# A gated conv and gMLP decoder layer in split fp32: loads of the first stage in a written order, the second half's row statistics from a token-major copy and spread through memory, weight remainders of v on GpSimd

## The chip, the cores and the metric

The kernel runs on one core of a Trainium2 chip. The metric is device time in microseconds (us) of one execution, and of a set of executions the median. The engines are PE (TensorE; PEld is its weight load), DVE (VectorE), ACT (ScalarE), POOL (GpSimd) and SP, which here only issues DMAs.

## The reference

One layer on `x` of 2048 tokens by 1024 channels, all in fp32, with a conditioning vector `c`:

```python
mod = c @ w_ada + b_ada
shift, scale, gate = split(mod, 3)
h = rmsnorm(x, g_pre) * (1 + scale) + shift
p = h @ w_in            # 8 parts of 1024 columns
y_a = conformer_conv(p[A.val], p[A.glu], p[A.silu])
v = layernorm(gelu(p[B.v]));  u = gelu(p[B.u])
y_b = (u * (tril(W_s) v + b_s) * silu(p[B.silu])) @ w_sgu_out
merged = sigmoid(p[gA]) * y_a + sigmoid(p[gB]) * y_b
out = rmsnorm(x + gate * (merged @ w_o), g_final)
```

`y_a` is a GLU, a causal depthwise convolution of width 31, a LayerNorm, a SiLU gate and a projection; the mixing by `W_s` goes per head in chunks of 128 tokens. What matters here is the head of this: the adaLN shift and scale, the RMS norm of x, and the product of h with the 1024 columns of v.

## The kernel before

The tokens go through in two passes (`s`) of 1024, each in two halves of T = 512. Channels are cut in KT = 8 tiles `k` of 128, a half in NC = 4 chunks `c` of 128 tokens. Every fp32 product is made of three fp32r products: each operand is split in a high part (a copy on ACT, L87) and a remainder (original minus high part, L88), and hi·hi, hi·lo and lo·hi are summed in PSUM. A step of the first stage is therefore 24 matmuls of 128x512: 4 chunks by 2 column halves by 3.

**The first stage (L455 to L563)** makes v for the first half of pass 0. It is written inside `tc.manual_schedule(engines=MANUAL)`, where PE, DVE, ACT and POOL run their instructions in the order in which the code is written. SP is not among them: its DMAs are put in order by the framework's scheduler. The stage does this:

- Loads: `xn` (x transposed, 8 tiles; L329), the row of c (`crow`), which PE multiplies by a column of ones to spread it over 128 partitions (L470, L473: `cbc`), per step two `wa` tiles of 512 KB (shift and scale weights, L381) and two pieces of the v weights (`raw`, 256 KB each, L174).
- Statistics of the first half: squares on ACT (L478, L481), a sum on DVE (L482), sums over partitions on PE (`col_sums`, L144), root and reciprocal (`rstd_cols`, L137, L138), and `spread` (L154, L161), which puts the 512 factors on all partitions by a diagonal and a matmul with ones.
- Per step k: `ada(k)` makes the shift and scale columns by two reductions of 128x1024 on DVE (L387) and an add (L391); `scaled(k)` multiplies xn by the row factors (L492); `shifted(k)` applies scale and shift twice on ACT (`modulated`, L352), once into the high part h, once in place; DVE makes the remainder of h (L516). The v weights are split on ACT (L87) and DVE (L88), a step ahead. Then 16 matmuls with the high part of h (L539, L540), 8 with its remainder (L544). Eight PSUM banks (`first`) hold the sums.
- The last step, k = 7, goes bank by bank (L552 to L554); `evict(u)` (L511) takes a bank through Gelu and gathers LayerNorm statistics.
- Beside it the second half's row statistics: squares of the transposed xn on ACT in steps 4 to 7 (L532), adds on DVE (L547, L548), `col_sums` after bank u = 5, then `spread` to `rx1`. `make_h` (L358, L352, L362) makes h of the second half, k = 0 in the stage, k = 1 to 7 behind it.

**Behind the stage** `v_pass` makes v of the second half from `A[1]`, once per column half n: 8 weight pieces of 12 matmuls each (L312 to L314). Its pieces are made by `make_row`, which splits them on ACT and DVE and sends each to memory (`d_wv`, issued on POOL, L186) for pass 1. The Gelu of column half n = 0 (L408) frees the banks for n = 1. Then follow the LayerNorm of v, the mixing, and the large products by quads (L297 to L303), whose order both versions share. `make_row` also makes the 16 pieces of `w_o`.

Three rings set what can run ahead: split weights `whl` (AHEAD + 1 = 5 tiles), `raw` (8), and the large ring `hs` (28 tiles of 512 KB), which holds h, wa, vn and the squares. Weights are prepared in the order of their use by `prep_to` and `take`.

Of the kernel before, what the change touches and what calls it, by code (L numbers as in the profile page):

```python
# [40 lines left out]
def hybrid_layer(  # L41
# [130 lines left out]
    def raw(mat, key, src):  # L172
        t = wp.tile([P, T], F32, tag="raw", name="raw", bufs=8)
        nc.sync.dma_start(out=t, in_=src)  # L174
        raws[key] = t
        return t

    def piece_tile():
        return wp.tile([P, 2, T], F32R, tag="whl", name="whl", bufs=AHEAD + 1)

    def make_row(mat, cache, k, n):
        def prep():
            w = piece_tile()
            split(w, raw(mat, None, mat[k * P : (k + 1) * P, n * T : (n + 1) * T]))
            if cache:
                nc.gpsimd.dma_start(  # L186
                    out=cache[k][n], in_=w.bitcast(F32).rearrange("p s c -> p (s c)")
                )
            return w

        return prep
# [185 lines left out]
    def load_ada(k):  # L377
# [4 lines left out]
            wa.append(t)  # L382
        return wa

    def ada(k, wa):
        for i in range(2):
            nc.vector.tensor_tensor_reduce(  # L387
                out=wa[i], in0=wa[i], in1=cbc, scale=col(V_GPRE, k) if i else 1.0, scalar=0.0,
                op0=ALU.mult, op1=ALU.add, accum_out=mod[:, k, i : i + 1],
            )  # L390
        nc.vector.tensor_tensor(out=mod[:, k], in0=mod[:, k], in1=base[:, k], op=ALU.add)  # L391


    def v_norm(vn, mv):
# [57 lines left out]


    xn = [xtile("xn") for _ in range(KT)]
    crow = row("crow")  # L455
    nc.sync.dma_start(out=crow[0:1, :], in_=rows[:, 3 * D : 4 * D])
    A = [[], []]
    load_xn(0, 0, xn)
    wa = {0: load_ada(0)}
    cbc = hs32("cbc")  # L460
    vn_first, st_first = v_tiles()
    with tc.manual_schedule(engines=MANUAL):
        nc.vector.tensor_copy(out=base[:, :, 0], in_=vec[:, V_BSH : V_BSH + KT])
        nc.vector.scalar_tensor_tensor(
            out=base[:, :, 1], in0=vec[:, V_BSC : V_BSC + KT], scalar=1.0,
            in1=vec[:, V_GPRE : V_GPRE + KT], op0=ALU.add, op1=ALU.mult,
        )
        for n in range(2):
            pt = bank()
            nc.tensor.matmul(  # L470
                pt, ones[0:1, :], crow[0:1, n * T : (n + 1) * T], start=True, stop=True
            )
            nc.scalar.activation(cbc[:, n * T : (n + 1) * T], pt, AF.Copy)  # L473
        acc = t512("acc")
        for k in range(KT):
            v = xn[k][:, :T]
            if k == 0:
                nc.scalar.activation(acc, v, AF.Square)  # L478
            else:
                q = t512("q")  # L480
                nc.scalar.activation(q, v, AF.Square)  # L481
                nc.vector.tensor_tensor(out=acc, in0=acc, in1=q, op=ALU.add)  # L482
        pc = bank()
        col_sums(acc, pc, 0, NC)
        prx = spread(rstd_cols(pc[:, :NC], NC), pc)
        rx = t512("rx")
        nc.scalar.activation(rx, prx, AF.Copy)
        ada(0, wa[0])

        def scaled(k):  # L490
            v = xn[k][:, :T]
            nc.vector.tensor_tensor(out=v, in0=v, in1=rx if k else prx, op=ALU.mult)  # L492

        def shifted(k):
            v = xn[k][:, :T]
            t = hs("h")
            modulated(t[:, 0], v, k)
            modulated(v, v, k)
            A[0].append(t)

        scaled(0)
        shifted(0)
        prep_to(2)
        cvt = wide()
        first = [bank() for _ in range(6)] + [cvt[:, :T], cvt[:, T:]]
        sq = []

        def evict(u):
            c, n = u // 2, u % 2
            vs = vn_first[c][:, n * T : (n + 1) * T]  # L510
            nc.scalar.activation(vs, first[u], AF.Gelu)  # L511
            nc.vector.bn_stats(out=st_first[c][:, n, :], in_=vs)

        for k in range(KT):
            t, v = A[0][k], xn[k][:, :T]
            nc.vector.tensor_tensor(  # L516
                out=t[:, 1], in0=v, in1=t[:, 0].bitcast(F32), op=ALU.subtract
            )
            ws = [ready.pop(0) for _ in range(2)]
            state["use"] += 2  # L520
            if k + 1 < KT:
                wa[k + 1] = load_ada(k + 1)
                scaled(k + 1)
                ada(k + 1, wa[k + 1])
                prep_to(2 * k + 4)
                shifted(k + 1)
            if k == 2:
                load_xn(0, 1, xn)
            if k >= 4:
                sq.append(hs32("q"))  # L530
                for i in range(2):
                    nc.scalar.activation(  # L532
                        sq[-1][:, i * T : (i + 1) * T], xn[2 * (k - 4) + i][:, T:S], AF.Square
                    )
            if k + 1 < KT:
                for u in range(2 * NC):
                    c, n = u // 2, u % 2
                    xh = t[:, 0, c * P : (c + 1) * P]
                    nc.tensor.matmul(first[u], xh, ws[n][:, 0], start=k == 0, stop=False)  # L539
                    nc.tensor.matmul(first[u], xh, ws[n][:, 1], start=False, stop=False)  # L540
                for u in range(2 * NC):
                    c, n = u // 2, u % 2
                    xl = t[:, 1, c * P : (c + 1) * P]
                    nc.tensor.matmul(first[u], xl, ws[n][:, 0], start=False, stop=False)  # L544
        tt = nc.vector.tensor_tensor
        for i in (1, 2, 3):
            tt(out=sq[0], in0=sq[0], in1=sq[i], op=ALU.add)  # L547
        tt(out=sq[0][:, :T], in0=sq[0][:, :T], in1=sq[0][:, T:], op=ALU.add)  # L548
        for u in range(2 * NC):
            c, n = u // 2, u % 2  # L550
            cs = slice(c * P, (c + 1) * P)
            nc.tensor.matmul(first[u], t[:, 0, cs], ws[n][:, 0], start=False, stop=False)  # L552
            nc.tensor.matmul(first[u], t[:, 0, cs], ws[n][:, 1], start=False, stop=False)
            nc.tensor.matmul(first[u], t[:, 1, cs], ws[n][:, 0], start=False, stop=True)  # L554
            if u < 2:
                evict(u)
            if u == 5:
                pc = bank()
                col_sums(sq[0], pc, 0, NC)
                c1 = rstd_cols(pc[:, :NC], NC)  # L560
        rx1 = spread(c1, pc)
        make_h(xn, rx1, 1, 0, A)
        for u in range(2, 2 * NC):  # L563
            evict(u)

    wsT = row("wsT")
    nc.sync.dma_start(out=wsT, in_=wst.rearrange("p j t -> p (j t)"))
# [22 lines left out]
    for s in range(NS):  # L590
        last = s + 1 == NS

        if s == 0:
            vn0, st0 = vn_first, st_first
            for k in range(1, KT):
                make_h(xn, rx1, 1, k, A)
        else:
            vn0, st0 = v_tiles()
# [532 lines left out]
```

## Time and profile before

| | |
|---|---|
| median of 3 runs | 1946.08 us (1945.91 to 1950.67) |
| profiled execution | 1949.32 us, of which the span is 1947.6 us |
| PE busy | 1859.1 us, 95% of the span |
| DVE, ACT, POOL busy | 1290.7, 867.6, 859.9 us |
| mean granted TensorE clock | 0.98 |
| DMA | 313.66 MB, mean 161 GB/s |

The span is the time between the profile's first and last instruction. A busy matmul of 128x512 at full clock comes every 0.22 to 0.23 us, though each lasts about 0.4: they overlap. Chain rows name what released each step of the path that ended last.

### The profile page before, as it was taken

How to read it: one execution, taken by the hardware profiler on the slowest of the kernel's cores; microseconds unless marked ns; L12 is line 12 of the kernel's file. 1: busy time of each engine (PE TensorE's matmuls, PEld its weight loads, DVE VectorE, ACT ScalarE, POOL GpSimd, SP SyncE). 2: the span in 40 equal slices, each digit the busy share in tenths (PEclk: the TensorE clock that was granted, in tenths of full speed). 3: DMA queues.
4: the chain of work that ended last, by engine and by line, in shares of the span. 5: the costliest groups of instructions: out<-in, count | busy, mean ns of one | idle time of the engine just before them, and what ended most of it. 6: DMA issues, size and time to landing. Idle time of an engine off the chain costs nothing.

```text
span 1947.6 us, 23204 instructions
## 1 busy us (share of the span) xinstructions
PE 1859.1 (95%) x8116; PEld 1517.4 (78%) x8116; DVE 1290.7 (66%) x1636; ACT 867.6 (45%) x1396; POOL 859.9 (44%) x734
## 2 busy tenths in 40 slices
PE   6798999999999998889999999999999999899998
PEld 4577888888888886668888878888888888677886
DVE  6776898888888127475851578889888861845424
ACT  4645555555546435322611455554555453532102
POOL 0035777777777710000100477777777774000000
PEclk9899999999999998889999999999999999899999
DMA  9562332222334384387886332333322246536484
GB/s 331 174 238 92 109 114 100 101 87 92 114 103 146 132 328 137 107 292 243 330 308 220 120 141 75 105 114 103 114 92 97 77 141 253 173 111 198 132 331 169
DMA packets 139015, 313.66 MB, mean 161 GB/s; under 512 B 15889, under 2 KB 16017, under 8 KB 138898
## 3 DMA queue, kind: packets, MB, share of 16 engines
q1 hardware_dynamic: 108434, 237.03, 36.2%
q0 software_dynamic: 11888, 41.43, 5.5%
q10 hardware_dynamic: 18576, 33.73, 4.6%
q8 instruction: 63, 1.03, 0.2%
q14 instruction: 54, 0.44, 0.1%
HBM read 226.66 MB, written 85.46 MB: 160 GB/s over the span
## 4 chain that ended last, share of the span: by engine, by line
PE 74%; issue 11%; DMA 7%; DVE 4%; ACT 3%; POOL 2%; SPq 0%; POOLq 0%; ACTq 0%; DVEq 0%
PE bank L297 21%; PE bank L300 21%; PE bank L303 21%; PE bank L312 3%; PE bank L313 3%; PE bank L314 3%; DMA wo<-d_wo 1%; PE bank L426 1%; DVE wa L387 1%; POOL whl L88 1%; DMA raw<-in_w_v 1%; DMA wa<-in_wada 1%; DMA xn<-in_xt 1%; DMA whl<-d_wo 1%; POOL raw L224 1%
## 5 line engine op out<-in xcount | busy, mean ns | idle before, releaser
L88 POOL TENSOR_TENSOR whl<-raw,whl 128x512 fp32r<-128x512 f32 x392 | 512.8, 1313 | 335.3 <-ACT whl L87 331.1
L704 DVE SCALAR_TENSOR_TENSOR cv<-a,vec,cv 128x1024 f32<-128x1024 f32 x464 | 596.6, 1286 | 31.6 <-ACT cv L698 21.4
L87 ACT ACTIVATE whl<-raw 128x512 fp32r<-128x512 f32 x504 | 314.3, 627 | 414.1 <-PE bank L303 214.7
L300 PE MATMUL bank<-s,whl 128*128 128x512 f32 x896 | 349.3, 390 | 1.7 <-DVE s L88 1.7
L303 PE MATMUL bank<-s,whl 128*128 128x512 f32 x896 | 349.7, 390 | 0.0
L297 PE MATMUL bank<-s,whl 128*128 128x512 f32 x896 | 349.4, 390 | 0.0
L224 POOL TENSOR_TENSOR raw<-raw 128x512 f32<-128x512 f32 x224 | 290.3, 1296 | 17.2
L297 PE MATMUL bank<-h,whl 128*128 128x512 f32 x672 | 264.0, 393 | 0.3 <-ACT bank L657 0.2
L300 PE MATMUL bank<-h,whl 128*128 128x512 f32 x672 | 261.8, 390 | 0.0
L303 PE MATMUL bank<-h,whl 128*128 128x512 f32 x672 | 261.6, 389 | 0.0
L300 PEld LDWEIGHTS bank<-s,whl 128*128 128x128 f32 x896 | 168.6, 188 | 38.0 <-DVE s L88 3.0
L297 PEld LDWEIGHTS bank<-s,whl 128*128 128x128 f32 x896 | 168.6, 188 | 34.9
L303 PEld LDWEIGHTS bank<-s,whl 128*128 128x128 f32 x896 | 168.7, 188 | 34.7
L297 PEld LDWEIGHTS bank<-h,whl 128*128 128x128 f32 x672 | 126.1, 188 | 32.5 <-DVE snap L680 5.3
L303 PEld LDWEIGHTS bank<-h,whl 128*128 128x128 f32 x672 | 126.1, 188 | 26.5
L300 PEld LDWEIGHTS bank<-h,whl 128*128 128x128 f32 x672 | 126.2, 188 | 25.6
L88 DVE TENSOR_TENSOR whl<-raw,whl 128x512 fp32r<-128x512 f32 x112 | 75.9, 688 | 96.9 <-ACT whl L87 91.8
L892 POOL DMA_DIRECT2D mb<-gl x32 | 17.3, 541 | 275.0 <-DVE gl L891 264.3
L297 PE MATMUL bank<-ya,whl 128*128 128x512 f32 x256 | 102.6, 401 | 13.8 <-ACT ya L87 10.6
L652 ACT ACTIVATE snap<-bank 128x512 f32<-128x512 f32 x112 | 66.5, 598 | 98.0 <-PE bank L303 98.0
L297 PE MATMUL bank<-yb,whl 128*128 128x512 f32 x256 | 105.4, 412 | 4.2 <-DVE gl L891 3.5
L300 PE MATMUL bank<-ya,whl 128*128 128x512 f32 x256 | 102.6, 401 | 1.4 <-DVE ya L88 1.4
(214 smaller groups left out, 2867.3 us busy)
## 6 DMA issues: line engine op xcount, KB each, us to landing
raw<-in_w_in SPq DMA_DIRECT2D x224, 256.0 KB, 3.0
yb<-yb SPq DMA_DIRECT2D x32, 512.0 KB, 7.6
whl<-d_wo SPq DMA_DIRECT2D x32, 512.0 KB, 4.6
whl<-d_wv SPq DMA_DIRECT2D x32, 512.0 KB, 4.3
xn<-in_xt SPq DMA_DIRECT2D x32, 256.0 KB, 5.4
wa<-in_wada SPq DMA_DIRECT2D x16, 512.0 KB, 6.5
raw<-in_w_v SPq DMA_DIRECT2D x32, 256.0 KB, 4.8
d_wv<-whl POOLq DMA_DIRECT2D x16, 512.0 KB, 6.5
```

The source lines that it names most:

```text
L87: nc.scalar.activation(hi, val, AF.Copy)
L88: eng.tensor_tensor(out=lo, in0=val, in1=hi.bitcast(F32), op=ALU.subtract)
L224: eng.tensor_tensor(out=dst, in0=dst, in1=src, op=ALU.add)
L297: nc.tensor.matmul(pt, wh, h[:, 0], start=start and k == 0, stop=False, skip_group_check=True)
L300: nc.tensor.matmul(pt, wh, h[:, 1], start=False, stop=False, skip_group_check=True)
L303: nc.tensor.matmul(pt, wl, h[:, 0], start=False, stop=k == last, skip_group_check=True)
L312: nc.tensor.matmul(pt, xh, w[:, 0], start=kt == 0, stop=False)
L313: nc.tensor.matmul(pt, xh, w[:, 1], start=False, stop=False)
L314: nc.tensor.matmul(pt, xl, w[:, 0], start=False, stop=kt == KT - 1)
L387: nc.vector.tensor_tensor_reduce(out=wa[i], in0=wa[i], in1=cbc, scale=col(V_GPRE, k) if i else 1.0, scalar=0.0, op0=ALU.mult, op1=ALU.add, ...
L652: nc.scalar.activation(t, pt, AF.Copy)
L704: nc.vector.scalar_tensor_tensor(out=dst, in0=a[:, k : k + S], scalar=col(V_CW, j * TAPS + k), in1=cv[0], op0=ALU.mult, op1=ALU.add,)
```

## The change

SP joins the engines of written order, and the loads are written out: xn on SP and ACT in turn, c's row spread by one broadcast DMA in place of PE and ACT, then `wa` and `raw` of steps 0 to 3, and four steps ahead from there (`load_step`). The table of the square root is loaded at the very start (`warm`). The reductions of step 0 are divided around the reciprocal, its weight splits stand ahead of h(0), the copy `rx` stands between the two modulations. The second half's statistics are taken from `sx`, four tiles of x with tokens on partitions, by a squaring with row sums on ACT in steps 4 and 5; root and reciprocal follow in step 5; POOL writes the 4 columns to memory (`d_rx`) and reads them back as a broadcast over all partitions (`rx1`). `make_h(1, 0)` and `(1, 1)` stand in step 6, `(1, 2)` after bank u = 3 of step 7. The adds, the `col_sums` and the `spread` of the second half go. `make_row` makes its remainders on POOL: 32 of w_v and 16 of w_o.

```diff
...
+    def raw_row(mat, k, n):
+        raw(mat, (id(mat), k, n), mat[k * P : (k + 1) * P, n * T : (n + 1) * T])
     def piece_tile():
...
             w = piece_tile()
-            split(w, raw(mat, None, mat[k * P : (k + 1) * P, n * T : (n + 1) * T]))
+            if (id(mat), k, n) not in raws:
+                raw_row(mat, k, n)
+            split(w, raws.pop((id(mat), k, n)), nc.gpsimd)
             if cache:
...
+    def ada_part(k, i, wa):
+        nc.vector.tensor_tensor_reduce(
+            out=wa[i], in0=wa[i], in1=cbc, scale=col(V_GPRE, k) if i else 1.0, scalar=0.0,
+            op0=ALU.mult, op1=ALU.add, accum_out=mod[:, k, i : i + 1],
+        )
+        if i:
+            nc.vector.tensor_tensor(out=mod[:, k], in0=mod[:, k], in1=base[:, k], op=ALU.add)
     def ada(k, wa):
         for i in range(2):
-            nc.vector.tensor_tensor_reduce(
-                out=wa[i], in0=wa[i], in1=cbc, scale=col(V_GPRE, k) if i else 1.0, scalar=0.0,
-                op0=ALU.mult, op1=ALU.add, accum_out=mod[:, k, i : i + 1],
-            )
-        nc.vector.tensor_tensor(out=mod[:, k], in0=mod[:, k], in1=base[:, k], op=ALU.add)
+            ada_part(k, i, wa)
...
     xn = [xtile("xn") for _ in range(KT)]
-    crow = row("crow")
-    nc.sync.dma_start(out=crow[0:1, :], in_=rows[:, 3 * D : 4 * D])
     A = [[], []]
-    load_xn(0, 0, xn)
-    wa = {0: load_ada(0)}
+    wa = {}
     cbc = hs32("cbc")
     vn_first, st_first = v_tiles()
-    with tc.manual_schedule(engines=MANUAL):
+    d_rx = scratch("d_rx", [1, T])
+    with tc.manual_schedule(engines=MANUAL | {ET.SP}):
+        warm = sm.tile([P, 8], F32, tag="cols", name="warm")[:, :1]
+        nc.scalar.activation(warm, eps_t, AF.Sqrt)
+        for k in range(KT):
+            (nc.scalar if k % 2 else nc.sync).dma_start(
+                out=xn[k][:, :T], in_=xt[k * P : (k + 1) * P, :T]
+            )
+        nc.sync.dma_start(out=cbc, in_=rows[:, 3 * D : 4 * D].broadcast_to([P, D]))
+        def load_step(k):
+            wa[k] = load_ada(k)
+            for n in range(2):
+                raw_row(w_v, k, n)
+        for k in range(4):
+            load_step(k)
         nc.vector.tensor_copy(out=base[:, :, 0], in_=vec[:, V_BSH : V_BSH + KT])
...
         )
-        for n in range(2):
-            pt = bank()
-            nc.tensor.matmul(
-                pt, ones[0:1, :], crow[0:1, n * T : (n + 1) * T], start=True, stop=True
-            )
-            nc.scalar.activation(cbc[:, n * T : (n + 1) * T], pt, AF.Copy)
         acc = t512("acc")
...
         col_sums(acc, pc, 0, NC)
+        ada_part(0, 0, wa[0])
         prx = spread(rstd_cols(pc[:, :NC], NC), pc)
-        rx = t512("rx")
-        nc.scalar.activation(rx, prx, AF.Copy)
-        ada(0, wa[0])
+        ada_part(0, 1, wa[0])
+        prep_to(2)
...
-        def shifted(k):
+        def shifted(k, between=None):
             v = xn[k][:, :T]
...
             modulated(t[:, 0], v, k)
+            if between:
+                between()
             modulated(v, v, k)
...
+        rx = t512("rx")
         scaled(0)
-        shifted(0)
-        prep_to(2)
+        shifted(0, lambda: nc.scalar.activation(rx, prx, AF.Copy))
         cvt = wide()
         first = [bank() for _ in range(6)] + [cvt[:, :T], cvt[:, T:]]
-        sq = []
+        sx = []
+        ssx = sm.tile([P, NC], F32, tag="oss", name="ssx")
+        def square(i):
+            nc.scalar.activation(sx[i], sx[i], AF.Square, accum_out=ssx[:, i : i + 1])
...
             state["use"] += 2
+            if k + 4 < KT:
+                load_step(k + 4)
+            if k == 0:
+                for c in range(NC):
+                    sx.append(hs32("sx"))
+                    nc.sync.dma_start(out=sx[c], in_=x[T + c * P : T + (c + 1) * P, :])
+            if k + 5 == KT:
+                load_xn(0, 1, xn)
             if k + 1 < KT:
-                wa[k + 1] = load_ada(k + 1)
                 scaled(k + 1)
...
                 shifted(k + 1)
-            if k == 2:
-                load_xn(0, 1, xn)
-            if k >= 4:
-                sq.append(hs32("q"))
+            if k in (4, 5):
+                square(2 * k - 8)
+                square(2 * k - 7)
+            if k == 5:
+                c1 = rstd_cols(ssx, NC)
+                rx1 = t512("rx1")
+                nc.gpsimd.dma_start(out=d_rx.rearrange("o (c p) -> (o p) c", p=P), in_=c1)
+                nc.gpsimd.dma_start(out=rx1, in_=d_rx.broadcast_to([P, T]))
+            if k == 6:
                 for i in range(2):
-                    nc.scalar.activation(
-                        sq[-1][:, i * T : (i + 1) * T], xn[2 * (k - 4) + i][:, T:S], AF.Square
-                    )
+                    make_h(xn, rx1, 1, i, A)
             if k + 1 < KT:
...
                     nc.tensor.matmul(first[u], xl, ws[n][:, 0], start=False, stop=False)
-        tt = nc.vector.tensor_tensor
-        for i in (1, 2, 3):
-            tt(out=sq[0], in0=sq[0], in1=sq[i], op=ALU.add)
-        tt(out=sq[0][:, :T], in0=sq[0][:, :T], in1=sq[0][:, T:], op=ALU.add)
         for u in range(2 * NC):
...
             nc.tensor.matmul(first[u], t[:, 1, cs], ws[n][:, 0], start=False, stop=True)
-            if u < 2:
-                evict(u)
-            if u == 5:
-                pc = bank()
-                col_sums(sq[0], pc, 0, NC)
-                c1 = rstd_cols(pc[:, :NC], NC)
-        rx1 = spread(c1, pc)
-        make_h(xn, rx1, 1, 0, A)
-        for u in range(2, 2 * NC):
             evict(u)
+            if u == 3:
+                make_h(xn, rx1, 1, 2, A)
...
             vn0, st0 = vn_first, st_first
-            for k in range(1, KT):
+            for k in range(3, KT):
                 make_h(xn, rx1, 1, k, A)
...
```

The diff leaves unsaid how the written order falls on the queues. On SP, before, around the loads of step 6 (`wa_563` and `wa_565`; `raw_791` to `raw_809` are weights of the pass behind the stage):

```order
L381 DMA wa_468<-in_wada 128x1024
L381 DMA wa_470<-in_wada 128x1024
L174 DMA raw_621<-in_w_v 128x512
L174 DMA raw_626<-in_w_v 128x512
L381 DMA wa_514<-in_wada 128x1024
L381 DMA wa_516<-in_wada 128x1024
L174 DMA raw_791<-in_w_v 128x512
L174 DMA raw_797<-in_w_v 128x512
L174 DMA raw_803<-in_w_v 128x512
L174 DMA raw_809<-in_w_v 128x512
L381 DMA wa_563<-in_wada 128x1024
L381 DMA wa_565<-in_wada 128x1024
```

On SP now, the loads of step 4 (`wa_343`) and step 5 (`wa_397`):

```order
L386 DMA wa_343<-in_wada 128x1024
L386 DMA wa_345<-in_wada 128x1024
L174 DMA raw_347<-in_w_v 128x512
L174 DMA raw_349<-in_w_v 128x512
L548 DMA sx_351<-in_x 128x1024
L548 DMA sx_353<-in_x 128x1024
L548 DMA sx_355<-in_x 128x1024
L548 DMA sx_357<-in_x 128x1024
L386 DMA wa_397<-in_wada 128x1024
L386 DMA wa_399<-in_wada 128x1024
L174 DMA raw_401<-in_w_v 128x512
L174 DMA raw_403<-in_w_v 128x512
```

Behind the stage's first loads no weight of the next pass stands ahead of a `wa` any more; the last of those and the second half of xn come behind step 7's `raw`.

On DVE, before, step 7's column add, its weight remainders, the remainder of h(7) (`h_630`), then the second half's sums:

```order
L391 TENSOR_TENSOR mod_87<-mod_87,base_88 128x2
L88 TENSOR_TENSOR whl_620<-raw_621,whl_620 128x512
L88 TENSOR_TENSOR whl_625<-raw_626,whl_625 128x512
L516 TENSOR_TENSOR h_630<-xn_227,h_630 128x512
L547 TENSOR_TENSOR q_535<-q_535,q_584 128x1024
L547 TENSOR_TENSOR q_535<-q_535,q_633 128x1024
L547 TENSOR_TENSOR q_535<-q_535,q_661 128x1024
L548 TENSOR_TENSOR q_535<-q_535 128x512
```

On DVE now, from the same add (`h_643`, `h_648` are h of the second half, k = 0 and 1; `h_639` is the remainder of h(7)):

```order
L396 TENSOR_TENSOR mod_87<-mod_87,base_88 128x2
L363 TENSOR_TENSOR xn_220<-xn_220,rx1_601 128x512
L363 TENSOR_TENSOR xn_223<-xn_223,rx1_601 128x512
L363 TENSOR_TENSOR xn_224<-xn_224,rx1_601 128x512
L363 TENSOR_TENSOR xn_225<-xn_225,rx1_601 128x512
L367 TENSOR_TENSOR h_643<-xn_220,h_643 128x512
L363 TENSOR_TENSOR xn_221<-xn_221,rx1_601 128x512
L363 TENSOR_TENSOR xn_226<-xn_226,rx1_601 128x512
L363 TENSOR_TENSOR xn_227<-xn_227,rx1_601 128x512
L367 TENSOR_TENSOR h_648<-xn_221,h_648 128x512
L538 TENSOR_TENSOR h_639<-xn_227,h_639 128x512
```

The remainder of h(7) moved behind seven multiplications by `rx1` and two remainders of the second half.

On POOL, before, from the start of the program: nothing of the first stage but the mask of `wsT` and the weight writes:

```order
L110 AFFINE_SELECT ident_81<-ident_81 128x128
L571 AFFINE_SELECT wsT_725<-wsT_725 128x1024
L575 DMA d_ws_89<-wsT_725 128x1024
L186 DMA d_wv00_92<-whl_790 128x1024
L186 DMA d_wv10_94<-whl_796 128x1024
L186 DMA d_wv20_96<-whl_802 128x1024
```

On POOL now, at step 5 (`whl_633`, `whl_636` are step 7's weight remainders, `whl_778` and later those of the next pass):

```order
L88 TENSOR_TENSOR whl_590<-raw_449,whl_590 128x512
L562 DMA d_rx_237<-cols_598 128x4x1
L88 TENSOR_TENSOR whl_778<-raw_779,whl_778 128x512
L191 DMA d_wv00_92<-whl_778 128x1024
L563 DMA rx1_601<-d_rx_237 128x512
L88 TENSOR_TENSOR whl_633<-raw_493,whl_633 128x512
L88 TENSOR_TENSOR whl_636<-raw_495,whl_636 128x512
L88 TENSOR_TENSOR whl_784<-raw_785,whl_784 128x512
L191 DMA d_wv10_94<-whl_784 128x1024
L88 TENSOR_TENSOR whl_790<-raw_791,whl_790 128x512
L191 DMA d_wv20_96<-whl_790 128x1024
```

The read of `rx1` stands behind one remainder and one weight write, and the weight remainders of step 7 stand behind the read.

On ACT now, behind the last Gelus of the stage (`xn_227` is the last modulation of the second half; L405 is the root of the LayerNorm, L417 the Gelu of the pass behind the stage):

```order
L357 ACTIVATE h_750<-xn_227,mod_87 128x512
L405 ACT_TABLE_LOAD
L405 ACTIVATE rs_759<-mv_754,eps_t_84 128x4
L357 ACTIVATE xn_227<-xn_227,mod_87 128x512
L87 ACTIVATE whl_802<-raw_803 128x512
L87 ACTIVATE whl_820<-raw_821 128x512
L87 ACTIVATE whl_838<-raw_839 128x512
L87 ACTIVATE whl_856<-raw_857 128x512
L87 ACTIVATE whl_874<-raw_875 128x512
L87 ACTIVATE whl_892<-raw_893 128x512
L87 ACTIVATE whl_910<-raw_911 128x512
L87 ACTIVATE whl_928<-raw_929 128x512
L417 ACT_TABLE_LOAD
L417 ACTIVATE vn_766<-bank_774 128x512
```

As before, the Gelu of column half n = 0 stands behind splits of later weights, down to `whl_928`, the fourth piece of column half n = 1.

## Rows read from the trace of the kernel before

**Rows 1.** Busy time by stretch; us, busy PE, PEld, DVE, ACT, POOL, PEclk, DMA, GB/s.
```profile
10.00:20.00 10.00, 3.92 (x10) 2.29 (x10) 6.88 (x13) 3.46 (x6) 0.00 (x0) 1.00 1.04 397
22.00:62.00 40.00, 35.39 (x144) 27.67 (x144) 31.89 (x56) 16.90 (x27) 2.15 (x2) 1.00 0.77 277
200.00:220.00 20.00, 20.00 (x90) 16.56 (x89) 18.88 (x21) 12.42 (x20) 14.16 (x11) 1.00 0.49 159
```

**Rows 2.** Chain of waits, 50 to 120 us: start us, us, what.
```profile
53.26 5.41 DMA wa<-in_wada
...
66.47 4.58 DMA raw<-in_w_v
...
75.47 0.80 PE bank L554
...
80.11 0.43 PE bank L552
...
87.73 1.28 ACT L511
...
89.02 3.04 ACT vn L511 x6
...
92.06 1.38 ACT h L352 x2
...
108.63 0.53 POOL d_wv L186
...
109.23 6.53 DMA d_wv<-whl
...
118.52 0.50 PE bank L312
```

**Rows 3.** Timeline, 0 to 31 us: start us, us, engine, line, what, [idle before <- releaser].
```profile
5.12 2.00 SPq L381 DMA_DIRECT2D wa<-in_wada  x2
...
15.65 0.18 DVE L138 RECIPROCAL cols<-cols 128x4 f32<-128x4 f32 x1 [2.26 <-ACT cols L137]
...
22.44 0.79 PE L539 MATMUL bank<-whl,h 128*128 128x512 f32 x1 [3.62 <-ACT whl L87]
...
29.78 0.39 PE L539 MATMUL bank<-whl,h 128*128 128x512 f32 x1
```

**Rows 4.** Timeline, 36 to 43 us, DVE and ACT rows of one step.
```profile
36.66 0.69 DVE L516 TENSOR_TENSOR h<-xn,h 128x512 fp32r<-128x512 f32 x1 [0.52 <-ACT xn L352]
...
37.27 0.68 DVE L492 TENSOR_TENSOR xn<-xn,rx 128x512 f32<-128x512 f32 x1
...
40.53 0.82 ACT L352 ACTIVATE h<-xn,mod 128x512 fp32r<-128x512 f32 x1 [2.87 <-DVE mod L391]
...
42.10 1.14 ACT L87 ACTIVATE whl<-raw 128x512 fp32r<-128x512 f32 x2
...
42.24 0.69 DVE L516 TENSOR_TENSOR h<-xn,h 128x512 fp32r<-128x512 f32 x1 [0.53 <-ACT xn L352]
```

**Rows 5.** Tile wa, 0 to 30 us: its DMAs.
```profile
DMA to landing us min/median/max: 6.0/7.5/7.8
```

**Rows 6.** Page, costliest groups: busy us, mean ns | idle before, releaser.
```profile
L88 POOL TENSOR_TENSOR whl<-raw,whl 128x512 fp32r<-128x512 f32 x392 | 512.8, 1313 | 335.3 <-ACT whl L87 331.1
```

**Rows 7.** Groups on ACT, shapes apart: busy us, mean ns | idle before.
```profile
L978 ACT ACTIVATE junk<-xo 128x1024 bf16<-128x1024 f32 x12 | 12.6, 1047 | 66.8 <-DVE xo L962 66.6 <-ACT junk L978 0.2
...
L978 ACT ACTIVATION_READ_ACCUMULATOR junk<-xo 128x1 f32 x12 | 2.2, 187 | 0.0
...
L137 ACT ACTIVATE cols<-oss,eps_t 128x4 f32<-128x4 f32 x3 | 0.9, 297 | 0.1
```

**Rows 8.** Page, DMA queues: packets, MB, share of 16 engines.
```profile
q0 software_dynamic: 11888, 41.43, 5.5%
```

**Rows 9.** DMA issues: count, KB each, median us to landing.
```profile
r<-r POOLq DMA_DIRECT2D x32, 256.0 KB, 3.2
```

**Rows 10.** Tile d_wv: its DMAs.
```profile
DMA to landing us min/median/max: 4.2/6.5/10.4
```

## The prediction

> **What bounds the kernel now.** The page says PE 95% busy. The edits lie in the first 120 us, so the windows come first [rows 1]: at 200 to 220 us PE takes a matmul every 0.222 us (90 in 20.00) and is full; at 22 to 62 us it runs 144 matmuls, six steps of 24 that would need 32 us, in 40. So the first stage has gaps, and what closes them counts one to one as long as no later wait takes it up. Next the chain of waits there [rows 2]: a step waits 5.41 us for a `wa` load (53.26) and 4.58 us for a `raw` (66.47); PE's last step begins late (75.47), its first matmuls 0.43 us apart; behind the stage ACT has a table load, evictions and modulations to do (87.73 to 92.06); a weight's write to memory of 6.53 us (109.23) ends last before PE's third bank of the second column half starts at 118.52. That instant is my mark: behind it the two programs order their work alike. Last the timeline of the start [rows 3] and of one undisturbed step [rows 4], for the pace.
>
> **The pace.** From one remainder of h to the next it is 5.58 us (36.66 to 42.24) [rows 4]; 24 matmuls at 0.222 to 0.23 are 5.3 to 5.5. On DVE each step needs h's remainder, xn times the factors, two reductions and two weight remainders; h's remainder still waits 0.52 us for ACT. Moving the weight remainders to POOL therefore gives the step nothing: the next wait is the same one on ACT, and PE's own 5.4 to 5.5 stands just behind. I cost that edit at 0 in the stage. The cover is POOL's idle time, two remainders of 1.31 us [rows 6] in 5.5 us.
>
> **Part by part, in times from the span's start.**
>
> *Start.* PE's first matmul is at 22.44 [rows 3], behind the weight splits. Those now stand ahead of h(0), so h(0) ends the wait: at best 20.4 (−2.0). Against it: `wa` of step 0 now has cbc, wsT and its write ahead, 1.57 MB more, at 397 GB/s [rows 1] 3.9 us. Issued at 5.12 and landing in up to 7.8 [rows 3, 5], it comes at 12.9 + 3.9 = 16.8, while one reduction now stands ahead of the reciprocal that was at 15.65. Two reductions lie between 37.27 + 0.60 and 40.53 [rows 4], at most 1.33 each; with 1.25 the worst is 22.8 (+0.4). I take 22.1, near the worst, since the bytes are certain. The root's table load hid behind the column sums; its move is worth 0.
>
> *Steps 0 to 6.* The first step takes 7.34 us (22.44 to 29.78), later ones 5.4 to 5.5. About 18.0 MB must land up to `wa` of step 7. At 390 GB/s that is done near 50 us, at the 277 GB/s of [rows 1] near 62, and it is needed near 61. So both load waits go. Step 1 starts at 29.4, step 6 at 56.5, its high part is done by 60.3.
>
> *Statistics.* ACT finishes xn(6) at 57.0, then squares twice, priced by the same shape at the end of the kernel: 1.05 + 0.19 each, 2.5; the root is 0.30 [rows 7]. Root done 59.8, reciprocal 60.0. h's remainder of step 6 stands behind that on DVE, 60.6, so step 6 ends at 62.4 instead of 61.8: a new wait, about 0.6.
>
> *The round trip through memory* has no row of its own. The nearest is POOL's queue: 3.2 us for a 256 KB write [rows 9]; the longest seen is 10.4 [rows 10]. `d_rx`: 60.0 + 3.2 = 63.2. POOL meanwhile makes one remainder and issues a weight write (0.53 [rows 2]), until 63.3. The read: 63.3 + 3.2, plus 0.5 for 512 small elements, lands at 67.0. Ends: 65.3 if small transfers are quicker, 74.4 with 10.4 for the read. I take 67.0, since [rows 9] has the same queue and the read's size.
>
> *What queues behind it.* On DVE the remainder of h(7) now stands behind seven multiplications by `rx1` and two remainders, each 0.60 us from start to start, as 36.66 to 37.27 shows [rows 4]; the second remainder also waits for ACT's two modulations. That ends at 73.0, and h(7)'s remainder at 73.6. PE's h(7) is ready at 64.7; it does two matmuls and stands until 73.6. Before, it went on at 75.47 [rows 2]. Of about 10 us won in loads, 8 are lost to this new wait: the gain here is only 1.9.
>
> *From step 7 to the mark.* Before, matmuls were 0.43 apart at first (80.11) [rows 2], 12 of them or 5.1 us. I keep that: 19 matmuls for seven banks end at 80.4 (12 at 0.43, 7 at 0.23). No column sums or spread interrupt them (about 1.9 us gone). Two weight pieces and the eighth bank, 51 − 24 = 27 matmuls, to 86.5; two more pieces to 92.0. The fifth piece (`whl_802`) waits for ACT: from 79.75 (xn of k = 2) it has 12 modulations at 0.69 to 0.82, I take 0.71 [rows 2, 4], 4 evictions at 0.51 (3.04 / 6), table 1.28, root 0.30 and two splits at 0.55 (1.14 / 2) [rows 2, 4, 7], 13.3 in all: 93.0. POOL's remainder makes it 94.3. That is a gap of 2.3 on PE. The pass ends near 104.5.
>
> Then the Gelu that frees the banks stands behind `whl_928`, which takes the ring place of the seventh piece and waits until that piece is in memory. POOL needs 2 x 1.31 + 2 x 0.53 = 3.7 us per pair; the write is issued at 99.3 and lands 6.5 later [rows 10], 105.8. Split 0.55, table 1.28, Gelu 0.52: PE's third bank at **108.2**, against 118.52. Gain **10.3**.
>
> *Behind the mark.* 16 remainders of w_o move to POOL: a piece feeds 12 matmuls, 2.7 us, POOL needs 1.31 + 0.53 for it, so 0. If POOL were behind there, each piece would cost at most 1.31 less 0.68, the same shape on DVE [rows 4], 0.6, 10 us in all; I see no queue ahead of it long enough.
>
> **Sum.** 1947.6 − 10.3 = 1937.3 of span. The median of 1946.08 is 1.5 below the profiled span (execution 1949.32), so **1936.0 us** (1946.08 − 10.3 = 1935.8). Bounds: start −1.7/+0.7, round trip −1.7/+7.4, write landing −2.3/+3.9 (4.2 and 10.4 [rows 10]). The first two mostly move together with the third: what step 7 loses, the write's wait partly hides. The forecast's own range is 1931 to 1940.
>
> **A rule against this change.** At 200 to 220 us DVE is busy 18.88 us and POOL 14.16 of the same 20 [rows 1], so they overlap for at least 13 us, and POOL's remainder keeps 1.31 us over 392 [rows 6]. The sum by that row stands as above. The Trainium skill, "SBUF — State Buffer", § Who interferes with whom, says that a DVE instruction with two SBUF inputs and GpSimd's reading exclude each other. By that rule moving remainders to GpSimd would only queue them before DVE; this trace does not agree with it for these shapes.
>
> **Rivals.**
>
> 1. *DVE and POOL exclude each other in the stage.* Then of two remainders one fits DVE's wait in the step and the other adds 1.3 us to a period. Six steps: +7.8, 1943.8, within 0.3% of before. The overlap above speaks against it; the stage has other instructions on DVE (reductions), which speaks for it. 0.05. This is what the Trainium skill's rule of the last paragraph would do here.
> 2. *A late round trip.* If read or write take what the longest POOL write took (10.4 [rows 10]), the first remainder of h(7) comes 6 to 7 us later, and ACT's evictions and modulations with it: 1942. For: the loads of the next pass are on the queues then. Against: the rates are lower by then. 0.13, no change.
> 3. *Slower: the small elements go one by one.* `d_rx` is 128 x 4 single numbers. POOL's queue took 11888 packets in 5.5% of 16 engines' span [rows 8]: 0.055 x 16 x 1947.6 / 11888 = 0.144 us each. All 512 on one engine are 74 us, and h(7) waits for all of them: −10.3 + 70 = +60, 2006. Spread over 16 engines they are 4.6, 4.1 above my 0.5: about 1940. It turns the sign if the round trip takes over 7 + 10 + 6 = 23 us. For: nothing else in the trace writes single numbers. Against: the page's queue shares show work spread over all engines. 0.06. The Trainium skill, "DMA: Bandwidth & Descriptors", § Rules for kernel authors, says that a last dimension that isn't contiguous becomes one descriptor per element; no row here shows such a write, and the rule leaves open on how many engines they go.
> 4. *Faster still.* PE's matmuls of step 7 stay 0.22 apart (−2.5), the write lands in 4.2 (−2.3), the start gains 1.7: near 1929.5. 0.12.
>
> **How the numbers follow.** The forecast has 0.64. A measurement tells from no change what exceeds 0.3%, 5.8 us: faster is below 1940.2, slower above 1951.9. Faster: forecast 0.62 of 0.64 and rival 4, 0.12: 0.74. Same: rivals 1 and 2 and the forecast's edge, 0.19, a part of rival 3 (16 engines) among it. Slower: 0.07, the rest of rival 3 and a POOL queue that holds w_o. The range leaves out the slow case and most of rival 4: 1930.5 to 1943.0.
>
> **What will show it.** No wait for `wa` or `raw` between 29 and 62 us; steps 5.4 to 5.6 apart; DVE waiting for `rx1` for 3 to 5 us before its first multiplication, near 67; PE standing from about 65 to 73.6 in step 7 and matmuls 0.43 apart behind it; the column sums of the second half gone; ACT's Gelu released by a weight write; PE's third bank at 108. I am wrong if the wait for `rx1` exceeds 10 us, if steps take 6.5 us or more, if waits for POOL's remainders appear before the fifth piece or among the w_o pieces, or if a gain at the mark is taken back later, in the mixing or the first quads.

## The result, and the profile after

The change made the kernel slower: 1962.29 us median of 5 runs (1955.46 to 1968.39) against 1946.65 before (5 runs), a ratio of 1.0076, 95% interval 1.0048 to 1.0104. The forecast was 1936.0, with a range up to 1943.0. From the page of the changed kernel, the span and the busy times:

```profile
span 1960.6 us, 23171 instructions
...
PE 1852.4 (94%) x8102; PEld 1513.4 (77%) x8102; DVE 1287.8 (66%) x1583; ACT 863.0 (44%) x1392; POOL 932.7 (48%) x784
```

The busy time by stretch of the changed kernel, columns as in [rows 1]:

```profile
22.00:62.00 40.00, 32.92 (x125) 25.26 (x125) 30.32 (x36) 14.49 (x23) 14.91 (x10) 0.96 0.95 359
62.00:84.00 22.00, 12.03 (x47) 8.31 (x45) 9.35 (x15) 10.92 (x20) 9.57 (x8) 0.84 0.20 56
84.00:118.00 34.00, 21.37 (x85) 16.75 (x86) 26.18 (x40) 22.15 (x33) 10.24 (x11) 0.81 0.35 120
```

At 22 to 62 us PE did 125 matmuls where it did 144 before [rows 1], though data came at 359 GB/s instead of 277: the loads were no longer late, and PE still did less. At 62 to 84 us it was busy 12 of 22 us, at 56 GB/s, so it waited for no bulk data there; the granted clock, 0.84 and 0.81 in the last two rows, fell with these stands (0.50, the lower of its two levels, at 84 to 94 us, where PE ran nothing). One step of the changed kernel, the timeline of DVE, then of POOL:

```profile
38.39 0.69 DVE L538 TENSOR_TENSOR h<-xn,h 128x512 fp32r<-128x512 f32 x1 [1.73 <-ACT xn L357]
39.00 1.80 DVE L508 TENSOR_TENSOR xn<-xn,rx 128x512 f32<-128x512 f32 x1
40.72 2.31 DVE L391 CUSTOM_DVE_ANT_0 wa<-wa,cbc 128x1024 f32<-128x1024 f32 x1
...
42.96 1.27 DVE L391 CUSTOM_DVE_ANT_0 wa<-wa,cbc,vec 128x1024 f32<-128x1024 f32 x1
...
46.17 0.69 DVE L538 TENSOR_TENSOR h<-xn,h 128x512 fp32r<-128x512 f32 x1 [1.74 <-ACT xn L357]
```

```profile
38.96 2.99 POOL L88 TENSOR_TENSOR whl<-raw,whl 128x512 fp32r<-128x512 f32 x2 [4.79 <-ACT whl L87]
46.73 2.97 POOL L88 TENSOR_TENSOR whl<-raw,whl 128x512 fp32r<-128x512 f32 x2 [4.78 <-ACT whl L87]
```

The remainder of h at 38.39 and 46.17 gives steps of 7.78 us; it was 5.58 [rows 4]. The multiplication L508 takes 1.80 us where L492 took 0.68 [rows 4], and the first reduction L391 takes 2.31 where the second beside it takes 1.27. Both start while the two POOL remainders run (38.96 to 41.95). The reading, tested below: DVE's instruction starts, stands while POOL works, then runs. The chain of waits in step 7 and behind it:

```profile
71.13 9.71 DMA d_rx<-cols
...
81.13 5.15 DMA rx<-d_rx
...
86.30 3.61 DVE xn L363 x4
...
93.55 0.61 DVE h L538
...
94.21 0.79 PE bank L582
...
120.86 6.37 DMA d_wv<-whl
...
129.99 0.50 PE bank L317
```

PE's longest waits there (in total, times, longest):

```profile
PE bank L582 <- DVE h L538: 10.4, 1, 10.4
PE bank L581 <- POOL whl L88: 6.0, 1, 6.0
```

The write of the factors took 9.71 us, their read 5.15, the remainder of h(7) ended at 94.1, and PE's third bank started at 129.99, 11.5 us after 118.52 [rows 2]. The wait of 6.0 us for step 7's weight remainders, which stand behind the read on POOL, cost nothing more, since the wait for h(7) ended later. From the first matmul of the mixing to the end, the profiled runs took 1817.0 us before (130.6 to 1947.6) and 1816.9 after (143.7 to 1960.6): all of the 13.0 us between these two executions lie in front of that.

### The profile page after: what moved, and what is told of

The parts are those of the page before. It is cut to its first block, busy times and chain, and to the rows that moved or that the text cites. A ratio compares the mean times of both kernels' runs of the same rounds, so it can differ in the third digit from the quotient of the medians.

```text
span 1960.6 us, 23171 instructions
## 1 busy us (share of the span) xinstructions
PE 1852.4 (94%) x8102; PEld 1513.4 (77%) x8102; DVE 1287.8 (66%) x1583; ACT 863.0 (44%) x1392; POOL 932.7 (48%) x784
## 2 busy tenths in 40 slices
DMA packets 139845, 316.54 MB, mean 161 GB/s; under 512 B 16016, under 2 KB 16144, under 8 KB 139728
## 4 chain that ended last, share of the span: by engine, by line
PE 76%; DMA 8%; issue 6%; DVE 5%; ACT 2%; POOL 2%; SPq 0%; POOLq 0%; ACTq 0%; DVEq 0%
PE bank L302 21%; PE bank L308 21%; PE bank L305 21%; PE bank L317 4%; PE bank L319 4%; PE bank L318 4%; POOL whl L88 2%; DMA xs<-in_x 2%; PE bank L435 1%; DMA wo<-d_wo 1%; DVE cv L725 1%; DVE rsq L864 1%; DMA whl<-d_wo 1%; DMA raw<-in_w_v 1%; DMA d_rx<-cols 0%
## 5 line engine op out<-in xcount | busy, mean ns | idle before, releaser
L88 POOL TENSOR_TENSOR whl<-raw,whl 128x512 fp32r<-128x512 f32 x440 | 583.3, 1331 | 464.1 <-ACT whl L87 402.7
L302 PE MATMUL bank<-ya,whl 128*128 128x512 f32 x256 | 102.0, 398 | 14.1 <-ACT ya L87 10.7
L302 PE MATMUL bank<-yb,whl 128*128 128x512 f32 x256 | 104.6, 409 | 4.1 <-DVE gl L912 3.4
L305 PE MATMUL bank<-yb,whl 128*128 128x512 f32 x256 | 102.4, 400 | 0.0
```

The costliest lines, as they stand in the source:

```text
L88: eng.tensor_tensor(out=lo, in0=val, in1=hi.bitcast(F32), op=ALU.subtract)
L302: nc.tensor.matmul(pt, wh, h[:, 0], start=start and k == 0, stop=False, skip_group_check=True)
L305: nc.tensor.matmul(pt, wh, h[:, 1], start=False, stop=False, skip_group_check=True)
```

## Experiments

Two costs were seen: longer steps (theory L: DVE and POOL exclude each other) and the round trip through memory with the order behind it (theory M). The column "mixing" is when PE's first matmul of the mixing starts in the profiled run; the ratio is to the kernel before, run again beside it on the same chip (1949.0 to 1951.1 us for the experiments), so medians of different rows are not to be divided.

| run | median us | ratio, 95% interval | mixing |
|---|---|---|---|
| before / the change | 1946.65 / 1962.29 | 1.0076 (1.0048 to 1.0104) | 130.6 / 143.7 |
| e1 remainders on DVE | 1948.75 | 0.9988 (0.9975 to 1.0002) | 130.5 |
| e4 before, remainders on POOL | 1963.98 | 1.0055 (1.0037 to 1.0073) | 140.6 |
| e2 other DVE instruction | 1966.09 | 1.0069 (1.0054 to 1.0084) | 144.1 |
| e3 round trip from SP | 1966.36 | 1.0064 (1.0040 to 1.0088) | 143.1 |
| e8 e1, write in 16-byte runs | 1943.32 | 0.9973 (0.9959 to 0.9986) | 126.3 |
| e5 e1, h(7) before the factors | 1933.13 | 0.9932 (0.9909 to 0.9955) | 118.0 |
| e7 e5, squares earlier | 1929.56 | 0.9914 (0.9890 to 0.9937) | 117.2 |
| e9 e7 and e8 | 1935.59 | 0.9943 (0.9921 to 0.9965) | 115.9 |
| e11 e5 and e8 | 1931.86 | 0.9904 (0.9885 to 0.9923) | 117.6 |

**e1 and e4: the remainders alone, taken back and put in.** e1 is the change with

```diff
-            split(w, raws.pop((id(mat), k, n)), nc.gpsimd)
+            split(w, raws.pop((id(mat), k, n)))
```

> The change with the 48 weight remainders of make_row back on DVE; all else as changed. Theory L (a plain tensor_tensor or reduction on DVE and a remainder on POOL, all from SBUF, exclude each other): L508 0.7 us instead of 1.8, the first reduction 1.2 instead of 2.3, steps 5.6 us instead of 7.78; six steps give 13 us, some of it lost in longer waits for the round trip; PE's third bank near 117 instead of 130, median 1947 to 1951. Theory M (the loss is the round trip through memory and the order behind it; steps are long for another reason, such as the load rate): steps stay near 7.8, median 1960.

A step of e1, DVE:

```profile
40.30 0.69 DVE L508 TENSOR_TENSOR xn<-xn,rx 128x512 f32<-128x512 f32 x1
40.91 1.22 DVE L391 CUSTOM_DVE_ANT_0 wa<-wa,cbc 128x1024 f32<-128x1024 f32 x1
...
43.45 1.29 DVE L88 TENSOR_TENSOR whl<-raw,whl 128x512 fp32r<-128x512 f32 x2
45.27 0.69 DVE L538 TENSOR_TENSOR h<-xn,h 128x512 fp32r<-128x512 f32 x1 [0.52 <-ACT xn L357]
```

L508 is 0.69, the reduction 1.22, and steps are 5.57 us (39.70 to 45.27). The mixing starts 13.2 us earlier than in the change. PE's longest wait in step 7 and behind:

```profile
PE bank L582 <- DVE h L538: 17.1, 1, 17.1
```

So e1 reaches step 7 early, stands 17.1 us there, and its mixing starts where that of the kernel before did. e4 is the kernel before with the remainders of `make_row` on POOL and nothing else:

> The kernel before with one part of the change alone: make_row's 48 remainders on POOL. Theory L: the steps grow from 5.6 towards 7.8, but the two load waits of 5.4 and 4.6 us hide part of it: PE's third bank 3 to 9 us later than 118.5, median 1950 to 1956. Theory M: no change, 1946 to 1947.

Its steps show the same pair (POOL, then DVE):

```profile
58.51 2.98 POOL L88 TENSOR_TENSOR whl<-raw,whl 128x512 fp32r<-128x512 f32 x2 [6.29 <-ACT whl L87]
58.56 1.78 DVE L492 TENSOR_TENSOR xn<-xn,rx 128x512 f32<-128x512 f32 x1
...
60.27 2.31 DVE L387 CUSTOM_DVE_ANT_0 wa<-wa,cbc 128x1024 f32<-128x1024 f32 x1
```

Where the next `wa` is in time, a step grows to 7.77 us (57.95 to 65.72). PE's third bank starts at 125.68, 7.2 us later than before, as theory L had it; the mixing starts 10.0 later, and the ratio is worth 10.7 us (1946.65 x 0.0055), a little above the 3 to 9 expected. The load waits of the kernel before hid a part, no more. Theory M alone is out.

**e2 and e10: what makes the two engines exclude each other.** In the trace of before one DVE row keeps its length under POOL, another does not (each fence: one stretch, DVE and POOL):

```profile
203.37 1.28 POOL L88 TENSOR_TENSOR whl<-raw,whl 128x512 fp32r<-128x512 f32 x1
203.37 2.60 DVE L704 SCALAR_TENSOR_TENSOR cv<-a,vec,cv 128x1024 f32<-128x1024 f32 x2
```

```profile
175.58 2.78 DVE L88 TENSOR_TENSOR s<-xn,s 128x512 fp32r<-128x512 f32 x2
...
176.51 1.29 POOL L88 TENSOR_TENSOR whl<-raw,whl 128x512 fp32r<-128x512 f32 x1
```

Two scalar_tensor_tensor of 128x1024 take 2.60 beside a POOL remainder, 1.30 each; two subtractions of 128x512, both operands in SBUF, take 2.78, not the 1.28 that a pair takes at 171.77. The first guess was the form of the instruction. e2 writes the stage's multiplication, reductions, column add and subtraction in the form that was not slowed:

```diff
-            nc.vector.tensor_tensor(out=v, in0=v, in1=rx if k else prx, op=ALU.mult)
+            nc.vector.scalar_tensor_tensor(
+                out=v, in0=v, scalar=1.0, in1=rx if k else prx, op0=ALU.mult, op1=ALU.mult
+            )
...
```

> The change with remainders on POOL, but the stage's DVE work (row factors, remainder of h, reductions, column add) written as scalar_tensor_tensor, which elsewhere in this trace runs beside POOL's remainders at its own length. Theory L with the exclusion hanging on the form of the DVE instruction: L508 0.7 us, reductions 1.2 to 1.3, steps 5.6, median 1946 to 1950. If any DVE instruction with two SBUF inputs is excluded, steps stay at 7.8 and the median at 1960; if the reductions in this form cost more, steps between.

```profile
39.02 2.99 POOL L88 TENSOR_TENSOR whl<-raw,whl 128x512 fp32r<-128x512 f32 x2 [4.79 <-ACT whl L87]
39.06 1.80 DVE L511 SCALAR_TENSOR_TENSOR xn<-xn,rx 128x512 f32<-128x512 f32 x1
...
40.78 2.31 DVE L391 SCALAR_TENSOR_TENSOR wa<-wa,cbc 128x1024 f32<-128x1024 f32 x1
```

1.80 and 2.31 again: the guess fell. What differs between the rows of before is where the operands lie: `cv` is a PSUM tile. e10 leaves the row factors in PSUM; for the bank that this takes it leaves out the eighth bank's products, so its time is not compared:

```diff
-            nc.vector.tensor_tensor(out=v, in0=v, in1=rx if k else prx, op=ALU.mult)
+            nc.vector.tensor_tensor(out=v, in0=v, in1=prx, op=ALU.mult)
...
-        first = [bank() for _ in range(6)] + [cvt[:, :T], cvt[:, T:]]
+        first = [bank() for _ in range(5)] + [cvt[:, :T], cvt[:, T:]]
```

> The change with one operand moved: the row factors stay in a PSUM bank, so that the multiplication L508 reads one SBUF tile and one PSUM bank; the reductions beside it still read two SBUF tiles. To free the bank, the eighth bank's 24 products (tokens 384 to 511, columns 512 to 1023) are left out, and its eviction takes the seventh bank's sums; the rx copy goes. If the exclusion is between a DVE instruction that reads two SBUF operands and POOL, L508 falls from 1.8 to 0.7 us while POOL runs, the first reduction still takes 2 us or more, and steps shorten by 0.3 to 1.1 us (the reduction now meets the first remainder). If any tensor_tensor is excluded, L508 stays at 1.8 and steps at 7.8. Its time is not comparable (21 matmuls a step).

```profile
37.02 3.50 POOL L88 TENSOR_TENSOR whl<-raw,whl 128x512 fp32r<-128x512 f32 x2 [3.58 <-ACT whl L87]
37.06 0.68 DVE L508 TENSOR_TENSOR xn<-xn,bank 128x512 f32<-128x512 f32 x1
...
37.66 1.73 DVE L391 CUSTOM_DVE_ANT_0 wa<-wa,cbc 128x1024 f32<-128x1024 f32 x1
...
39.32 2.29 DVE L391 CUSTOM_DVE_ANT_0 wa<-wa,cbc,vec 128x1024 f32<-128x1024 f32 x1
...
43.54 0.69 DVE L537 TENSOR_TENSOR h<-xn,h 128x512 fp32r<-128x512 f32 x1 [1.73 <-ACT xn L357]
```

The same multiplication, under the same POOL work, takes 0.68 us. The reductions, both inputs in SBUF, still take 1.73 and 2.29 (without POOL: 1.22 and 1.27), and the step is 7.09 us (36.45 to 43.54). So DVE's instruction stands when it reads two SBUF operands while POOL works on SBUF, and one PSUM operand frees it.

POOL can be the one that stands: its pair takes 3.50 us in e10. In the changed kernel a remainder that began under a running reduction took 2.00 us instead of 1.3, while the reduction kept its 1.22:

```profile
71.92 1.22 DVE L391 CUSTOM_DVE_ANT_0 wa<-wa,cbc 128x1024 f32<-128x1024 f32 x1
72.27 2.00 POOL L88 TENSOR_TENSOR whl<-raw,whl 128x512 fp32r<-128x512 f32 x1 [0.34 <-ACT whl L87]
```

**e3 and e8: the 9.7 us write.** e3 issues both DMAs of the round trip on SP:

> The change with both DMAs of the round trip issued on SP instead of POOL. If the 9.7 us of the write are POOL's queue (software descriptors), the write lands in 2 to 3 us, DVE's wait for rx1 shrinks from 10.7 to 3 to 4, median 5 to 7 below the change. If they are the 512 single numbers, the write stays at 8 to 10 us and the median within 2 us, less what POOL wins by not standing 6 us before step 7's remainders. Theory L alone expects steps of 7.8 as before.

The DMA issues of e3 (count, KB each, median us to landing):

```profile
rx<-d_rx SPq DMA_DIRECT2D x1, 256.0 KB, 6.5
...
d_rx<-cols SPq DMA_DIRECT2D x1, 2.0 KB, 9.5
```

9.5 us from SP too, so POOL's queue is not the cost, and the time stays that of the change. In e3's trace the pieces can be seen: 16512 DMA packets under 512 B, against 16016 in the change. On POOL's queue they cannot: e1 and e8 both have 16016, so there the number of pieces is read from the code. e8 is e1 with the columns written as 128 runs of 16 bytes; the multiplications read `rx1` with a stride:

```diff
...
-nc.gpsimd.dma_start(out=d_rx.rearrange("o (c p) -> (o p) c", p=P), in_=c1)
+nc.gpsimd.dma_start(out=d_rx.rearrange("o (p c) -> (o p) c", p=P), in_=c1)
...
```

> e1 with the 4 columns written to memory as 128 runs of 16 bytes instead of 512 single numbers (the factors then lie in another order in rx1, and the multiplications read them with a stride). If the 9.3 us of the write are counted by elements, it lands in 3 to 4 us (a quarter of 7 us plus a fixed 2), rx1 arrives 5 to 6 us earlier, median 3 to 5 below e1. If they are a fixed cost of a small write or of the queue, 9 us again and the median within 2 of e1. A multiplication with a stride that takes over 0.7 us would give part back.

```profile
rx<-d_rx POOLq DMA_DIRECT2D x1, 256.0 KB, 5.1
...
d_rx<-cols POOLq DMA_DIRECT2D x1, 2.0 KB, 2.2
```

2.2 us instead of e1's 9.3, for the same 2 KB from the same queue. The mixing starts 4.2 us earlier; the ratio falls from 0.9988 to 0.9973, but these intervals overlap. The single numbers are the cost: (9.3 − 2.2) / (512 − 128) is on average 18 ns for each further piece. The Trainium skill, "DMA: Bandwidth & Descriptors", § Rules for kernel authors, has one descriptor per element where the last dimension isn't contiguous; e3's packets and the two lengths agree with it. The stride has a price of its own, as the expectation allowed for: a multiplication by `rx1` takes 1.05 to 1.08 us in e8, 0.68 in e1.

**e5, e7, e9, e11: the order behind the factors.** e5 is e1 with the multiplications by `rx1` moved behind six evictions, so that the remainder of h(7) does not stand behind them:

```diff
...
-            if k == 6:
-                for i in range(2):
-                    make_h(xn, rx1, 1, i, A)
...
-            if u == 3:
-                make_h(xn, rx1, 1, 2, A)
+            if u == 5:
+                for i in range(KT):
+                    v = xn[i][:, T:S]
+                    nc.vector.tensor_tensor(out=v, in0=v, in1=rx1, op=ALU.mult)
+                for i in range(2):
+                    make_h(xn, None, 1, i, A)
+        for k in range(2, KT):
+            make_h(xn, None, 1, k, A)
...
```

> e1 (remainders on DVE, loads and round trip as changed) with one more edit: the remainder of h(7) and six evictions stand ahead of everything that needs rx1, the eight multiplications by rx1 follow in a row. If it was the order that gave the loads' gain away: PE's gap in step 7 falls from 17 to 20 us (64.5 to 82) to under 3, the wait moves behind the eighth bank and is 5 to 8 us there (rx1 lands near 74.7), the mixing starts 5 to 8 us before e1's 130.5, median 4 to 8 below e1. If the round trip itself is the bound whatever the order, or the later chain of modulations, the mixing starts within 2 us of e1's.

PE's waits of e5 from step 7 on (in total, times, longest):

```profile
PE bank L317 <- ACT h L357: 6.5, 1, 6.5
...
PE bank L580 <- DVE h L539: 1.4, 1, 1.4
```

The wait of 17.1 became 1.4 in step 7 and 6.5 behind it, and the mixing starts 12.5 us before e1's, more than the 5 to 8 expected. e7 is e5 with the squares in steps 2 and 3 and the round trip after step 3:

> e5 with the four squares two steps earlier (steps 2 and 3, where the token-major copy has landed) and the round trip after step 3. It then ends near 64 instead of 74.7, hidden by steps 4 to 6: no wait for rx1 anywhere, mixing 2 to 6 us before e5's. If ACT's squares in steps 2 and 3 lengthen these steps (4.2 us of ACT in two steps that have some 2.3 us of ACT to spare each), steps of 6 to 6.5 there eat 1 to 2 us. If behind the stage the modulations and weight writes bound it, the same as e5.

From e7's chain of waits:

```profile
51.99 12.04 DMA raw<-in_w_v
64.11 0.64 ACT whl L87
```

The write, now among the stage's loads, takes 13.0 us, and a weight load issued 3.8 us behind it lands after 12.04, where e1's loads land in 5.3 at that time, before its write. The mixing gains only 0.8 us, not 2 to 6. e9 and e11 add the 16-byte runs to e7 and to e5:

> e7 and e8 together: all three cures. If e7 has hidden the round trip, the write's form changes nothing more: within 1 us of e7. If e7 still waits, 3 to 5 below it.

> e5 (remainders on DVE, remainder of h(7) and evictions ahead of the rx1 work) with the write of the factors in 16-byte runs, squares where the change has them. The write then lands in 2 to 5 us, rx1 near 67 instead of 77.4, DVE's wait for rx1 of 4.2 us goes and PE's 6.5 us wait before the second half; mixing 3 to 6 us before e5's, median at e7's level, 1928 to 1932. If the modulations on ACT bound it, within 2 us of e5 (1933).

The loads of xn issued at 48 to 51.9 us, in e7 and then in e9:

```profile
DMA to landing us min/median/max: 12.1/12.1/12.9
DMA to landing us min/median/max: 5.4/5.4/6.6
```

The two kernels differ only in the write's form and in the stride of the multiplications, which run later; so the single numbers hold up other transfers. The write takes 4.8 us in e9 and 2.8 in e11, yet the mixing starts only 1.3 us before e7's and 0.4 before e5's. This does not show that the round trip's length has stopped mattering, because the stride takes the gain back. The eight multiplications in e5 and in e11, then e11's chain of waits:

```profile
77.41 4.91 DVE L585 TENSOR_TENSOR xn<-xn,rx 128x512 f32<-128x512 f32 x8 [4.22 <-DMA rx<-d_rx]
74.10 8.07 DVE L585 TENSOR_TENSOR xn<-xn,rx 128x512 f32<-128x512 f32 x8
```

```profile
77.07 5.09 DVE xn L585 x5
82.16 0.61 DVE h L368
82.82 2.07 PE bank L319 x4
```

e11 no longer waits for `rx1` and starts the eight 3.3 us earlier, but they take 3.2 us longer, and PE waits for a remainder of h behind them. What shorter writes give without the stride was not run. e9's median lies 6 us above e7's, where within 1 was expected. The four intervals of e5, e7, e9 and e11 overlap: each beats the kernel before, by 0.6 to 1.0%, and the change by more; which of them is best stays open.

## Why the prediction was wrong

**Loads: right.** No `wa` is waited for between 29 and 62 us, and with the remainders off POOL (e1) PE takes its steps without a gap: busy 40.00 of 40 us at 22 to 62. The first matmul came at 21.68, forecast 22.1.

**"Moving the weight remainders to POOL therefore gives the step nothing", cover and all: this step failed.** The edit was priced at 0 in the stage; it costs 2.2 us in most steps (7.78 against 5.58). Up to the end of the statistics' root, forecast at 59.8 and measured at 70.6, that is 10.8 us; e1 issues the write that follows it at 59.3, the change at 71.1. The overlap of DVE and POOL at 200 to 220 us [rows 1] was true but of another kind: every DVE instruction of that stretch has a PSUM tile (`cv` or a bank) among its operands. The mean of POOL's remainder [rows 6] could not show it either: it is 1331 ns even in the changed kernel, 1313 before, because mostly DVE is the one that stands. The rows of before that told of it were single ones (2.78 above). Rival 1 named the mechanism, and the Trainium skill, "SBUF — State Buffer", § Who interferes with whom, states it: two SBUF inputs on DVE against GpSimd reading SBUF. With that rule the traces agree, from before (2.78 for two) to e10 (0.68 against 1.80); the prediction's sentence that the trace does not was a misreading. The prediction gave it 0.05 and sized it at 1.3 a step: it let one remainder fit DVE's idle time, but ACT's split releases both just when DVE's multiplication is due, and DVE loses 1.1 to each.

**The round trip: the right place, the wrong size, and the second term that failed.** Forecast 7.0 us from the reciprocal to `rx1`, measured 15.5 (70.8 to 86.3). The write was priced at 3.2 by a large write [rows 9] and took 9.71; the read, priced at 3.2 and 0.5 for small elements (a term from no row), took 5.15. Rival 3's number for 16 engines, 4.6 on top, was nearer than the term used (e8 shows 7.1). Rival 2 came near the length of it (6 to 7 us on h(7)), by another cause. Behind it the four first multiplications took 3.61 instead of 2.4, under POOL again.

**What queues behind it: right.** h(7) did stand behind seven multiplications and two remainders, 94.1 instead of 73.6, and this order, not the loads, set the end of the stage. The 20.5 us are 10.8 from the steps, 8.5 from the round trip and 1.2 from the slowed DVE work. At the third bank 20.5 had become 21.8 (129.99 against 108.2). e5 shows the price of the order without the POOL remainders: 12.5 us.

**Behind the mark: nearly right.** From the third bank to the mixing the change takes 1.6 us more; its granted clock is 0.72 at 130 to 136 us, where the kernel before has 1.00 at 118 to 131. From the mixing on it is the same 1817 us to the end, so the remainders of w_o cost nothing that one execution shows; they were not tried apart.

**The signs of being wrong.** Three of the four came: a wait of 10.75 us for `rx1`, steps of 7.78, and PE's 6.0 us for POOL's remainders in step 7. The chances have a slip: 0.19 for no change is less than its named parts, 0.05, 0.13 and 0.02.

So without the POOL remainders the change is worth about 0 (e1), because the round trip and the order behind it ate what the loads gave; the POOL remainders made that a loss.

## What to carry to other kernels

Before work moves to GpSimd, look at the rows of single DVE instructions that ran under GpSimd, and split them by where their operands lie: a stretch in which both are busy proves nothing about SBUF operands if DVE was reading PSUM. A small write to memory cost here by the number of its pieces (512 or 128 for the same 2 KB); write runs, but count what the reader's stride then costs. Put everything that does not need the result of such a trip ahead of what does, on every queue in order. A fixed load order pays only if the next wait in the stage is moved too.

## What was not expected of the hardware

- An instruction that stands for the other engine is shown as busy: L508 at 1.80 us did 0.68 us of work. At 22 to 62 us DVE's busy time looks like work: 5.9 us a step (30.32 of 40 us, steps of 7.78), against 4.6 in e1 (33.29, steps of 5.57), which has the two remainders besides.
- An addition of two columns (L396, 128x2), 0.16 us alone, took 1.12 us where it met a POOL remainder (at 65.38).
- 2 KB in 512 single numbers land in 9.3 to 13.0 us, in 128 runs of 16 bytes in 2.2 to 4.8. Loads of 256 KB issued at 48 to 53 us, beside the write, take 12.0 to 12.9 us in e7 and 5.3 to 6.6 in e9.
- A multiplication of 128x512 that reads one operand with a step of 16 bytes takes 1.04 to 1.10 us (e8, e9, e11), without the step 0.68.
